# Fetched expert rows of 88 tokens in three sets of 64, 16 and 8: all dots first, then all sums, paced by the product

## The chip, the cores and the metric

The kernel runs on one core of a Trainium2 chip, in one launch. The metric is the device time of that core in microseconds (us), the median of several runs. PE is the matrix engine (TensorE), DVE the vector engine, ACT the scalar engine, POOL the GpSimd engine, which here issues the fetches by index, and SP the engine that issues the large loads. A weight load on PE is listed apart as PEld.

## The reference, cut to what matters

One decoder layer for 256 tokens of width 1024, all in float32: a mixer (attention heads beside recurrent heads), then PEER, then a last norm. The change touches PEER alone. Each token has 8 heads, and each head picks 16 of 16384 experts; an expert is one row of `peer_u` and one of `peer_v`, 4 KB each.

```python
def one(xb):
    qp = (xb @ wq).reshape(PEER_TOKEN_BLOCK, PEER_HEADS, 2, PEER_DKEY // 2)
    s = jnp.einsum('thcd,hcnd->thcn', ...)
    ...
    eidx = jnp.take_along_axis(cidx, p, axis=-1)          # 8 x 16 = 128 rows of each token
    gates = jax.nn.softmax(sc, axis=-1)
    ue = u[eidx]
    ve = v[eidx]
    act = jax.nn.gelu(jnp.einsum('td,thkd->thk', xb, ue), approximate=False)
    return jnp.einsum('thk,thkd->td', (gates * act), ve)
```

The layer ends with `h = h + peer(...)` and `out = rmsnorm(h)`.

## The kernel before

**Two ways for PEER.** 168 of the 256 tokens (`NP`) go the dense way: PE multiplies them with every row of `peer_u` and then of `peer_v`, and a matrix with the gates at the chosen experts (built in the tile `bigB`) picks out what counts. The other 88 tokens (`S`, the first 88) go by fetch: for each, the 128 chosen rows are fetched from memory by index. A fetch (`gissue`) brings 128 rows, one for each partition, 512 KB; 88 fetches bring rows of `peer_u` and 88 rows of `peer_v`, 176 in all.

**The dense stream.** It is a loop of 256 units: units 0 to 127 are the U half (`pu`, from S_U on), units 128 to 255 the V half (`py`, from S_V on). A unit takes one tile of 512 KB (`raw`), which SP loads eight units ahead, and does eight float32 matmuls with it. The trace has two records for each of these, so 16 records are one unit. In the U half ACT takes the results out of PSUM for every second unit with a Gelu (line 1149), one of them for two units. Between units 54 and 116 PE also builds the gate matrix (`gmm`, lines 1131 and 1132).

**The fetched tokens.** They stand in sets of 16 tokens, eight partitions to a token (the last has 8 tokens). For a fetch of kind "u" (`gdo`) DVE multiplies the fetched rows with the token rows (`xr`, loaded by `xload` from the copy `x_keep` in device memory, each row spread to its eight partitions) and adds up to one number for each partition; ACT takes the Gelu of a set's numbers; for a fetch of kind "v" DVE adds the weighted rows to `yacc`. When a set is done, two matmuls with a 0/1 matrix (`gsum`, line 1065) add the partitions of each token together on PE. The list `steps` sets the order: u of set 0, u of set 1, v of set 0, u of set 2, v of set 1, and so on, so a set's token rows are loaded when the set before last has its dots done.

**How the fetches are spread.** `gather(rate)` runs once in each unit. It adds the rate (`GU` 0.8 in the U half, `GV` 0.73 in the V half) to a counter; for every whole one, `gdo` is written for one fetch and `gissue` for the fetch seven places on (`LA` 8). Eight tiles hold fetched rows: four of the pool's tag "gt", four of the tag "sl". The first seven fetches are issued in unit 13 at once. In the V half a fetch also waits for the first matmul of the unit that it is written behind (`PS["pace"]`, a wait of POOL on PE); in the U half it waits for its tile and its turn only.

**The end.** `tail()` at the start of the V half issues four loads on POOL's queue: the residual rows of the dense tokens (three pieces of `h_keep`, into `fin`) and the last norm's vector, spread to all partitions. `gfinish` norms and stores the fetched tokens once the last `gsum` is done. After unit 255 the dense results are copied (`zcopy`), transposed (`ztrans`), normed (`finish`) and stored.

Each engine runs its instructions in the order in which this code writes them.

Of the kernel before, what the change touches and what calls it, by code (L numbers as in the profile page):

```python
# [9 lines left out]
F32 = mybir.dt.float32  # L10
# [3 lines left out]
U32 = mybir.dt.uint32  # L14
AF = mybir.ActivationFunctionType
OP = mybir.AluOpType
# [4 lines left out]
D = 1024  # L21
# [3 lines left out]
TAILN = 2  # L25
S = 88
NP = T - S
NSET = (S + 15) // 16
STEPS = [min(16, S - 16 * m) for m in range(NSET)]
TOP = NP // 2  # L30
R0 = TOP - 45

# [2 lines left out]
def block_kernel(ctx: ExitStack, tc: tile.TileContext, xT, x, lbl, recg, g1, g2, g2f, gf, skT,  # L35
                 w_in, w_out, wq, pu, pv, pur, pvr, out, dbg=None, last_step=None):
    nc = tc.nc
# [24 lines left out]
    S_OUT, S_WQ, S_U, S_V = 28, 36, 52, 180  # L62
    NS = 2 * len(units)
# [77 lines left out]
    for dc in range(8):  # L141
        g = g1t[:, dc:dc + 1]
# [108 lines left out]
    PS = {}  # L251
# [31 lines left out]
    acc = pre.tile([128, 2, 4, 32], F32)  # L283
# [427 lines left out]
    x_keep = dram.tile([128, D], F32)  # L711
# [49 lines left out]
    HN = {}  # L761
# [78 lines left out]
    def routing():  # L840
# [48 lines left out]
        ge = [gm[:, 512 * tt:512 * tt + 128].rearrange("p (n k) -> p n k", k=16) for tt in range(2)]  # L889
# [12 lines left out]
            nc.vector.tensor_mul(ge[tt], ge[tt], gs[tt][:, :, None].to_broadcast([128, 8, 16]))  # L902

        def packed():
            pk = GA["pk"]
            i12 = [PS["I12"][:, r, 0:128].rearrange("p (h a k) -> p h a k", h=8, a=2) for r in range(2)]
            nc.vector.scalar_tensor_tensor(pk[:, :, :, 0:8].bitcast(U32), i12[0], 128.0, i12[1], op0=OP.mult, op1=OP.add)
            nc.vector.tensor_copy(pk[:, :, :, 8:16], ge[0].rearrange("p h (a k) -> p h a k", a=2))
            for m in range(NSET):
                nc.gpsimd.dma_start(GA["pg", m], pk[16 * m:16 * m + STEPS[m]])  # L910
            GA["ready"] = True

        def slots():
# [47 lines left out]
    GA = {}  # L961

    def gather_open():
        gp = PS["gp"]
        GA["pk"] = gp.tile([128, 8, 2, 16], F32, name="pk")
        for m in range(NSET):
            GA["pg", m] = gp.tile([128, 2 * STEPS[m]], F32, name=f"pg{m}")
        GA["dot"] = gp.tile([128, NSET, 16], F32, name="dot")
        GA["w"] = gp.tile([128, NSET, 16], F32, name="gw")
# [4 lines left out]
        nc.vector.tensor_single_scalar(ri, ri, 3, op=OP.logical_shift_right)  # L974
        for n in (16, 8):
            GA["sel", n] = gp.tile([128, 2 * S], F32, name=f"sel{n}")
            nc.vector.tensor_tensor(GA["sel", n], ri, ci, op=OP.is_equal)
            if n == 16:
                nc.vector.tensor_single_scalar(ri, ri, 1, op=OP.logical_shift_right)
        xload(0)  # L980
        xload(1)

    def xload(m):
        if m >= NSET:
            return
        x_ = PS["gp"].tile([128, D], F32, name="xr", bufs=2)
        n = STEPS[m]
        hk = x_keep[16 * m:16 * m + n]
        nc.gpsimd.dma_start(x_, hk[:, None, :].to_broadcast([n, 128 // n, D]))
        GA["x", m] = x_  # L990

    steps = []
    for m in range(NSET):
# [9 lines left out]
    def gissue(j):  # L1003
        if j >= len(steps):
            return
        kind, m, k = steps[j]
        if j % 2:
            g = splp.tile([128, D], F32, name="gt", tag="sl")
        else:
            g = PS["gp"].tile([128, D], F32, name="gt", bufs=4)  # L1010
        i = nc.gpsimd.indirect_dma_start(g, None, pur if kind == "u" else pvr,  # L1011
                                         bass.IndirectOffsetOnAxis(GA["pg", m][:, k // 8 * 16 + k % 8:k // 8 * 16 + k % 8 + 1].bitcast(U32), 0))
        if "pace" in PS:
            tc.add_manual_dep(i.ins, PS["pace"].ins.name, PACE, reason="rows are fetched at the pace of the product")
        GA["g", j] = g

    def gdo(j):
        kind, m, k = steps[j]
        g = GA.pop(("g", j))
        if kind == "u":  # L1020
            x_ = GA["x", m]
            nc.vector.scalar_tensor_tensor(g, g, 1.0, x_, op0=OP.mult, op1=OP.mult,  # L1022
                                           accum_out=GA["dot"][:, m, k:k + 1])
            if k == STEPS[m] - 1:
                GA["gelu"] = [GLAG, m]
                xload(m + 2)
        else:
            w = GA["w"][:, m, k:k + 1]
            if k == 0:
                n = STEPS[m]  # L1030
                nc.vector.tensor_mul(GA["w"][:, m, 0:n].rearrange("p (a k) -> p a k", k=8),
                                     GA["dot"][:, m, 0:n].rearrange("p (a k) -> p a k", k=8),
                                     GA["pg", m].rearrange("p (a f) -> p a f", f=16)[:, :, 8:16])
# [4 lines left out]
            if k == STEPS[m] - 1:  # L1038
                GA["sum"] = [GLAG, m]

    GLAG = 5
# [8 lines left out]
    def gdot():  # L1050
        m = due("gelu")
        if m is not None:
            d = GA["dot"][:, m, 0:STEPS[m]]
            nc.scalar.activation(d, d, AF.Gelu)  # L1054

    def gsum():

        m = due("sum")
        if m is None:
            return  # L1060
        if m == 0:
            GA["p"] = [bank(psG, "pyg") for _ in range(2)]
        y = GA.pop(("y", m))
        for dh in range(2):
            nc.tensor.matmul(GA["p"][dh][0:S], GA["sel", STEPS[m]][:, S - 16 * m:2 * S - 16 * m],  # L1065
                             y[:, dh * 512:dh * 512 + 512], start=m == 0, stop=m == NSET - 1)
        if m == NSET - 1:
            GA["end"] = True

    def gfinish():  # L1070
        f = PS["gp"].tile([128, D], F32, name="fing", tag="xr", bufs=2)
        r = PS["gp"].tile([128, 8], F32, name="rg")
        nc.gpsimd.dma_start(f[0:S], h_keep[0:S, 0])
        jk = PS["gp"].tile([128, D], F32, name="jkg", tag="xr", bufs=2)
        for dh in range(2):
            c = slice(dh * 512, dh * 512 + 512)
            nc.vector.scalar_tensor_tensor(f[0:S, c], GA["p"][dh][0:S], 1.0 / GS, f[0:S, c], op0=OP.mult, op1=OP.add)  # L1077
        nc.scalar.activation(jk[0:S], f[0:S], AF.Square, accum_out=r[0:S, 0:1])  # L1078
        nc.scalar.activation(r[0:S, 1:2], r[0:S, 0:1], AF.Sqrt, bias=epst[0:S], scale=1.0 / D)
        nc.vector.reciprocal(r[0:S, 2:3], r[0:S, 1:2])  # L1080
        nc.vector.scalar_tensor_tensor(f[0:S], f[0:S], r[0:S, 2:3], HN["fin"][0:S, 2], op0=OP.mult, op1=OP.mult)
        nc.gpsimd.dma_start(out[0:S, 0], f[0:S])

    def gather(rate):
        if "ready" not in GA or gpos["do"] >= len(steps):
            return 0.0
# [150 lines left out]
    def pe(s):  # L1237
        if s < S_OUT:
            g, j = divmod(s, 4)
            n = ORD[g]  # L1240
            if n in ("f", "q", "qa", "ka"):
                p = bank(psA if n == "f" else psH, "pp")
# [22 lines left out]
        elif s < S_U:  # L1265
            j = s - S_WQ
            p = bank(psA, "pq")
            mm_col(s, p[:, 0:T], PS["hgH"], PS["hgL"], norm2_mid if j == 0 else None)
            ev(s + 1, ev_qp, j, p)
        elif s < S_V:  # L1270
# [131 lines left out]
```

## Time and profile before

| | |
|---|---|
| median of 3 runs | 841.32 us (840.7 to 842.4) |
| the profiled execution's own time | 845.24 us |
| its span, first to last instruction | 843.5 us |
| PE busy | 817.6 us (97% of the span) |
| DVE, ACT, POOL busy | 507.0, 248.2, 287.2 us |
| moved by DMA | 266.15 MB, 316 GB/s over the span |
| U half, V half on PE | from 197.9 us, from 524.4 us |

Busy time of PE is no measure by itself here, since a matmul that is stretched by a late weight load still counts as busy; the length of a unit tells whether PE is held up. The share of 16 DMA engines and the GB/s are in the same view as the busy times, by stretch.

### The profile page before, as it was taken

Reading aid. Unit: us, or ns where it says so; the run is one execution under the profiler, and the core shown is the slowest. Engines: PE = TensorE matmul, PEld = TensorE weight load, DVE = VectorE, ACT = ScalarE, POOL = GpSimd, SP = SyncE. Lnnn points to the kernel's source line nnn. Section 1 sums busy time; section 2 is a strip of 40 time slices with the busy share of each in tenths; the row PEclk is TensorE's granted clock in tenths of the full one; section 3 lists DMA queues with packets and bytes.
Section 4 is the critical chain, followed back from the end, with each engine's and each line's share of the span. In section 5 each row is a group of like instructions: output and inputs, shape, how many; then the busy total and the mean of one; then the engine's idle time right before and its main releaser. Section 6 shows DMA issues by size and latency. Waiting matters only on the chain.

```text
span 843.5 us, 15460 instructions
## 1 busy us (share of the span) xinstructions
PE 817.6 (97%) x6154; PEld 784.8 (93%) x6154; DVE 507.0 (60%) x1097; ACT 248.2 (29%) x565; POOL 287.2 (34%) x259
## 2 busy tenths in 40 slices
PE   6999999999999999999999999999999999999994
PEld 6987887999989899999999999998999999999994
DVE  6998576499998744777677765434433434334203
ACT  6853854742100214566455521000000000000003
POOL 3053001891284421433324234434533333233001
PEclk9999999999999999999999999999999999999998
DMA  8733335759699999999999999999999999999941
GB/s 312 241 110 102 125 112 191 232 190 325 206 379 409 371 408 408 370 402 370 336 362 338 401 357 382 342 338 409 409 403 407 408 400 401 363 405 402 320 125 50
DMA packets 73655, 266.15 MB, mean 316 GB/s; under 512 B 8751, under 2 KB 8839, under 8 KB 73199
## 3 DMA queue, kind: packets, MB, share of 16 engines
q1 hardware_dynamic: 45470, 164.29, 52.9%
q0 software_dynamic: 27824, 100.87, 31.9%
q8 instruction: 48, 0.79, 0.4%
q14 instruction: 25, 0.20, 0.1%
q10 hardware_dynamic: 288, 0.01, 0.0%
HBM read 262.42 MB, written 2.62 MB: 314 GB/s over the span
## 4 chain that ended last, share of the span: by engine, by line
PE 86%; DMA 7%; DVE 3%; issue 2%; ACT 1%; SPq 0%; ACTq 0%; DVEq 0%
PE pu L1277 33%; PE py L1288 33%; PE pa L214 4%; DMA raw<-in_pv 2%; DMA raw<-in_pu 2%; PE pw L226 2%; PE pq L200 2%; PE pq L201 2%; PE pq L203 2%; DVE sl L80 1%; DMA hT<-in_x 1%; PE pg L1132 1%; PE pyg L1065 1%; PE pg L1131 1%; PE psc L811 1%
## 5 line engine op out<-in xcount | busy, mean ns | idle before, releaser
L1277 PE MATMUL pu<-hn,raw 128*128 128x168 f32 x2048 | 301.5, 307 | 3.6 <-issue 1.6
L1288 PEld LDWEIGHTS py<-bigB,raw 128*128 128x128 f32 x2048 | 292.6, 190 | 9.7 <-DMA raw<-in_pv 6.0
L1288 PE MATMUL py<-bigB,raw 128*128 128x168 f32 x2048 | 298.9, 307 | 2.3 <-DMA raw<-in_pv 1.3
L1277 PEld LDWEIGHTS pu<-hn,raw 128*128 128x128 f32 x2048 | 292.9, 190 | 8.5 <-issue 6.9
L1037 DVE SCALAR_TENSOR_TENSOR yacc<-gt,gw,yacc 128x1024 f32<-128x1024 f32 x82 | 105.2, 1282 | 102.2 <-DMA gt<-in_pvr,pg 102.1
L1011 POOL DMA_INDIRECT gt<-in_pvr,pg x88 | 98.5, 1120 | 180.3 <-PE py L1288 104.5
L1011 POOL DMA_INDIRECT gt<-in_pur,pg x88 | 106.9, 1215 | 143.5 <-DVE gt L1022 48.4
L1022 DVE SCALAR_TENSOR_TENSOR gt<-gt,xr 128x1024 f32<-128x1024 f32 x88 | 106.5, 1222 | 57.0 <-DMA gt<-in_pur,pg 55.2
L1149 ACT ACTIVATE bigB<-pu 128x336 f32<-128x336 f32 (+22 forms) x57 | 21.7, 381 | 161.3 <-PE pu L1277 128.6
L80 DVE TENSOR_TENSOR sl<-raw,sh 128x1024 fp32r<-128x1024 f32 x37 | 52.6, 1427 | 16.9 <-ACT sh L79 16.3
L79 ACT CAST sh<-raw 128x1024 fp32r<-128x1024 f32 x51 | 53.1, 1052 | 14.5 <-PE pw L226 6.0
L1054 ACT ACTIVATE dot<-dot 128x16 f32<-128x16 f32 (+1 forms) x6 | 1.2, 208 | 187.7 <-DVE gt L1022 113.1
L1153 DVE TENSOR_TENSOR bigB<-tmp,bigB 128x336 f32<-128x336 f32 (+22 forms) x37 | 13.2, 357 | 54.0 <-ACT tmp L1152 47.8
L200 PE MATMUL pp<-XH,sh 128*128 128x256 f32 x128 | 32.4, 293 | 6.9 <-ACT sh L150 6.6
L80 POOL TENSOR_TENSOR sl<-raw,sh 128x1024 fp32r<-128x1024 f32 x14 | 33.2, 2388 | 2.2 <-ACT sh L79 2.1
L200 PEld LDWEIGHTS pp<-XH,sh 128*128 128x128 f32 x128 | 25.0, 196 | 7.5 <-ACT sh L150 6.6
L1078 ACT ACTIVATE jkg<-fing 88x1024 f32<-88x1024 f32 x1 | 1.1, 1057 | 104.9 <-DVE fing L1077 104.9
L201 PE MATMUL pp<-XL,sh 128*128 128x256 f32 x128 | 31.7, 288 | 0.0
L200 PE MATMUL pq<-hgH,sh 128*128 128x256 f32 x120 | 29.5, 286 | 0.0
L201 PE MATMUL pq<-hgL,sh 128*128 128x256 f32 x120 | 29.0, 281 | 0.0
L1115 ACT ACTIVATE rt<-iotaC,ni 128x128 f16<-128x128 f16 x88 | 27.6, 400 | 0.0
L201 PEld LDWEIGHTS pp<-XL,sh 128*128 128x128 f32 x128 | 25.1, 196 | 0.5 <-DVE XL L147 0.5
(300 smaller groups left out, 927.2 us busy)
## 6 DMA issues: line engine op xcount, KB each, us to landing
raw<-in_pu SPq DMA_DIRECT2D x128, 512.0 KB
raw<-in_pv SPq DMA_DIRECT2D x128, 512.0 KB
raw<-in_w_in SPq DMA_DIRECT2D x27, 512.0 KB
raw<-in_wq SPq DMA_DIRECT2D x16, 512.0 KB
raw<-in_w_out SPq DMA_DIRECT2D x8, 512.0 KB
xr<-x_keep POOLq DMA_DIRECT2D x6, 512.0 KB
gt<-in_pur,pg POOLq DMA_INDIRECT x88
gt<-in_pvr,pg POOLq DMA_INDIRECT x88
```

The lines of the kernel that those rows point to most:

```text
L79: nc.scalar.copy(h, r)
L80: (nc.gpsimd if s >= S_WQ + 2 else nc.vector).tensor_sub(lo, r, h.bitcast(F32))
L200: nc.tensor.matmul(p, hv[:, dc], xh[:, dc], start=(dc == 0), stop=False)
L201: nc.tensor.matmul(p, hv[:, dc], xl[:, dc], start=False, stop=False)
L214: nc.tensor.matmul(acc[tt], xx[:, dc, tt * 128:(tt + 1) * 128], w[:, c], start=(dc == 0 and w is hv and xx is xh), stop=(dc == 7 and w is lv))
L1011: i = nc.gpsimd.indirect_dma_start(g, None, pur if kind == "u" else pvr, bass.IndirectOffsetOnAxis(GA["pg", m][:, k // 8 * 16 + k % 8:k // ...
L1022: nc.vector.scalar_tensor_tensor(g, g, 1.0, x_, op0=OP.mult, op1=OP.mult, accum_out=GA["dot"][:, m, k:k + 1])
L1037: nc.vector.scalar_tensor_tensor(GA["y", m], g, w, GA["y", m], op0=OP.mult, op1=OP.add)
L1115: nc.scalar.activation(o2[:, k], iotaC, AF.Square, bias=RT["ni"][:, t0 + k:t0 + k + 1])
L1149: nc.scalar.activation(big[:, :, t:NP], p[:, :, t:NP], AF.Gelu)
L1277: nc.tensor.matmul(p, w[:, dc], HN["x"][:, dc], start=dc == 0, stop=dc == 7)
L1288: mm = nc.tensor.matmul(yacc(j), w[:, j * 128:j * 128 + 128], chunk(x), start=x == 0 and j % 2 == 0, stop=x == 127, skip_group_check=True)
```

## The change

There are three sets, of 64, 16 and 8 tokens: a token of the first has two partitions, one of the second eight, one of the third sixteen. The indices and the gates are no longer packed into one tile but sent as two (`pi`, `pg`), three small copies each. `steps` has all 88 dots first (u of sets 0, 1, 2), then all 88 sums (v of sets 0, 1, 2). The token rows of all three sets are loaded when the fetches' tiles are opened, at the start of the U half. Fetches of the U half also wait for the first matmul of their unit. The first seven fetches are issued two in a unit, in units 13 to 16. The rate of the V half is 0.77. `tail()` stands 16 units before the end of the stream.

```diff
-NSET = (S + 15) // 16
-STEPS = [min(16, S - 16 * m) for m in range(NSET)]
+SETS = [64, 16, 8]
+OFFS = [0, 64, 80]
+NSET = len(SETS)
...
             for m in range(NSET):
-                nc.gpsimd.dma_start(GA["pg", m], pk[16 * m:16 * m + STEPS[m]])
+                nc.gpsimd.dma_start(GA["pi", m], ki[OFFS[m]:OFFS[m] + SETS[m]])
+            for m in range(NSET):
+                nc.gpsimd.dma_start(GA["pg", m], kg[OFFS[m]:OFFS[m] + SETS[m]])
             GA["ready"] = True
...
-        xload(0)
-        xload(1)
+        for m in range(NSET):
+            xload(m)

     def xload(m):
-        if m >= NSET:
-            return
-        x_ = PS["gp"].tile([128, D], F32, name="xr", bufs=2)
-        n = STEPS[m]
-        hk = x_keep[16 * m:16 * m + n]
+        x_ = PS["gp"].tile([128, D], F32, name="xr", bufs=3)
+        n = SETS[m]
+        hk = x_keep[OFFS[m]:OFFS[m] + n]
         nc.gpsimd.dma_start(x_, hk[:, None, :].to_broadcast([n, 128 // n, D]))
         GA["x", m] = x_

-    steps = []
-    for m in range(NSET):
-        steps += [("u", m, k) for k in range(STEPS[m])]
-        if m:
-            steps += [("v", m - 1, k) for k in range(STEPS[m - 1])]
-    steps += [("v", NSET - 1, k) for k in range(STEPS[-1])]
+    steps = [(kind, m, k) for kind in "uv" for m in range(NSET) for k in range(SETS[m])]
...
-            if k == STEPS[m] - 1:
+            if k == SETS[m] - 1:
                 GA["gelu"] = [GLAG, m]
-                xload(m + 2)
...
-                GA["y", m] = PS["gp"].tile([128, D], F32, name="yacc", bufs=2)
+                GA["y", m] = PS["gp"].tile([128, D], F32, name="yacc", tag="xr", bufs=3)
...
-            nc.tensor.matmul(GA["p"][dh][0:S], GA["sel", STEPS[m]][:, S - 16 * m:2 * S - 16 * m],
+            nc.tensor.matmul(GA["p"][dh][0:S], GA["sel", m][:, S - OFFS[m]:2 * S - OFFS[m]],
                              y[:, dh * 512:dh * 512 + 512], start=m == 0, stop=m == NSET - 1)
...
     def gather(rate):
         if "ready" not in GA or gpos["do"] >= len(steps):
             return 0.0
-        while gpos["issue"] < min(gpos["do"] + LA - 1, len(steps)):
-            gissue(gpos["issue"])
-            gpos["issue"] += 1
-            if gpos["issue"] == LA - 1:
-                gpos["acc"] = -2.0
+        if gpos["issue"] < LA - 1:
+            for _ in range(2 if gpos["issue"] < LA - 2 else 1):
+                gissue(gpos["issue"])
+                gpos["issue"] += 1
+            if gpos["issue"] < LA - 3:
                 return 0.0
         gpos["acc"] += rate
...
             for dc in range(8):
-                nc.tensor.matmul(p, w[:, dc], HN["x"][:, dc], start=dc == 0, stop=dc == 7)
+                mm = nc.tensor.matmul(p, w[:, dc], HN["x"][:, dc], start=dc == 0, stop=dc == 7)
+                if dc == 0:
+                    PS["pace"] = mm
...
-    GU, GV = 0.8, 0.73
+    GU, GV = 0.8, 0.77
...
-        if s == S_V:
+        if s == NS - 16:
             tail()
```

On POOL, from the opening of the fetches' tiles on, the program before reads so (`xr` are the token rows, `pg` indices and gates, `gt` fetched rows, `fin` what the end needs; "x16" counts equal rows in a run):

```order
L989 DMA xr<-x_keep 128x1x1024 x2
...
L1011 DMA gt<-in_pur,pg_2418 128x1024 x16
L1011 DMA gt<-in_pur,pg_2419 128x1024 x6
L989 DMA xr<-x_keep 128x1x1024
L1011 DMA gt<-in_pur,pg_2419 128x1024 x10
...
L1011 DMA gt<-in_pur,pg_2421 128x1024 x16
L1164 DMA fin<-h_keep 40x1024
L1165 DMA fin<-h_keep 88x1024
L1166 DMA fin<-h_keep 40x1024
L1167 DMA fin<-in_gf 128x1024
L1011 DMA gt<-in_pvr,pg_2420 128x1024 x6
L989 DMA xr<-x_keep 128x1x1024
```

And the same queue in the changed program (its line 992 is `xload`, 1009 `gissue`, 1156 to 1159 `tail`):

```order
L992 DMA xr<-x_keep 128x1x1024 x3
L911 DMA pi_2419<-ki 128x1x64
...
L1009 DMA gt<-in_pur,pi_2419 128x1024 x64
L1009 DMA gt<-in_pur,pi_2423 128x1024 x16
L1009 DMA gt<-in_pur,pi_2427 128x1024 x8
L1009 DMA gt<-in_pvr,pi_2419 128x1024 x64
L1009 DMA gt<-in_pvr,pi_2423 128x1024 x16
L1009 DMA gt<-in_pvr,pi_2427 128x1024 x8
L1156 DMA fin<-h_keep 40x1024
L1157 DMA fin<-h_keep 88x1024
L1158 DMA fin<-h_keep 40x1024
L1159 DMA fin<-in_gf 128x1024
```

Four loads of token rows out of six stood between fetches, and now all three stand ahead of the first; the four loads for the end stood in the middle of the fetches and now stand behind the last.

On PE, from the last part of the U half to the last units, the program before (`pyg` is what `gsum` writes; eight instructions of `pu` or `py` are a unit):

```order
L1277 MATMUL pu<-hn,raw 128x168 x56
L1065 MATMUL pyg<-yacc,sel_2431 88x512 x2
L1277 MATMUL pu<-hn,raw 128x168 x48
L1288 MATMUL py<-bigB,raw 128x168 x296
L1065 MATMUL pyg<-yacc,sel_2431 88x512 x2
L1288 MATMUL py<-bigB,raw 128x168 x352
L1065 MATMUL pyg<-yacc,sel_2431 88x512 x2
L1288 MATMUL py<-bigB,raw 128x168 x256
L1065 MATMUL pyg<-yacc,sel_2431 88x512 x2
L1288 MATMUL py<-bigB,raw 128x168 x88
L1065 MATMUL pyg<-yacc,sel_2434 88x512 x2
L1288 MATMUL py<-bigB,raw 128x168 x20
```

And the changed program:

```order
L1269 MATMUL pu<-hn,raw 128x168 x88
L1282 MATMUL py<-bigB,raw 128x168 x680
L1057 MATMUL pyg<-yacc,sel_2436 88x512 x2
L1282 MATMUL py<-bigB,raw 128x168 x168
L1057 MATMUL pyg<-yacc,sel_2439 88x512 x2
L1282 MATMUL py<-bigB,raw 128x168 x88
L1057 MATMUL pyg<-yacc,sel_2442 88x512 x2
L1282 MATMUL py<-bigB,raw 128x168 x76
```

Six pairs of `pyg` (one more stands earlier in the U half of the program before) are now three, the first of them 85 units into the V half.

## Rows read from the trace of the kernel before

**Rows 1.** The page: busy time, share of the span and instructions of each engine.

```profile
PE 817.6 (97%) x6154; PEld 784.8 (93%) x6154; DVE 507.0 (60%) x1097; ACT 248.2 (29%) x565; POOL 287.2 (34%) x259
```

**Rows 2.** Chain that ended last: start us, us, engine and line, records.

```profile
403.77 1.72 PE pyg L1065 x4
...
616.91 100.32 PE py L1288 x704
...
818.71 1.72 PE pyg L1065 x4
```

**Rows 3.** Instructions of line 1065: durations in ns, first and last start.

```profile
L1065 PE MATMUL pyg<-yacc,sel x24: 592/592/592, 403.6 to 819.8; 128*88 128x512 f32 x24
```

**Rows 4.** Timeline of PE from the start of the V half: start us, us.

```profile
524.44 39.23 PE L1288 MATMUL py<-bigB,raw 128*128 128x168 f32 x272
564.69 2.55 PE L1288 MATMUL py<-bigB,raw 128*128 128x168 f32 x16 [1.02 <-DMA raw<-in_pv]
567.50 47.70 PE L1288 MATMUL py<-bigB,raw 128*128 128x168 f32 x304 [0.26 <-DMA raw<-in_pv]
615.03 1.88 PE L1065 MATMUL pyg<-yacc,sel 128*88 128x512 f32 x4
```

**Rows 5.** Timeline of ACT: the Gelu of every second unit of the U half.

```profile
230.90 0.45 ACT L1149 ACTIVATE bigB<-pu 128x336 f32<-128x336 f32 x1 [4.11 <-PE pu L1277]
...
256.40 0.45 ACT L1149 ACTIVATE bigB<-pu 128x336 f32<-128x336 f32 x1 [3.36 <-issue]
...
283.82 0.45 ACT L1149 ACTIVATE bigB<-pu 128x336 f32<-128x336 f32 x1 [4.11 <-PE pu L1277]
...
320.51 0.45 ACT L1149 ACTIVATE bigB<-pu 128x336 f32<-128x336 f32 x1 [4.68 <-PE pu L1277]
```

**Rows 6.** Stretches: busy us (records) of PE, PEld, DVE, ACT, POOL; clock; DMA share; GB/s.

```profile
198.00:230.00 32.00, 32.00 (x229) 32.00 (x228) 30.94 (x152) 7.91 (x12) 4.48 (x10) 1.00 0.78 250
250.00:280.00 30.00, 30.00 (x213) 30.00 (x212) 25.26 (x94) 3.15 (x7) 14.68 (x15) 1.00 1.03 409
282.00:290.00 8.00, 6.63 (x47) 6.32 (x46) 7.09 (x12) 3.67 (x5) 3.92 (x3) 1.00 1.03 316
530.00:538.00 8.00, 8.00 (x59) 8.00 (x58) 3.82 (x9) 0.22 (x1) 3.28 (x3) 1.00 1.03 265
552.00:564.00 12.00, 11.63 (x80) 11.12 (x78) 3.72 (x3) 0.00 (x0) 5.29 (x4) 1.00 1.04 290
...
524.00:543.00 19.00, 19.00 (x136) 19.00 (x135) 8.70 (x16) 3.44 (x5) 10.57 (x12) 1.00 0.99 322
543.00:616.00 73.00, 71.56 (x466) 66.46 (x466) 29.89 (x32) 0.00 (x0) 30.59 (x21) 1.00 1.03 388
616.00:790.00 174.00, 174.00 (x1211) 172.43 (x1210) 68.57 (x74) 0.42 (x2) 58.56 (x54) 1.00 1.02 397
790.00:825.00 35.00, 35.00 (x232) 32.89 (x231) 3.65 (x5) 2.73 (x4) 0.00 (x0) 1.00 0.52 164
```

**Rows 7.** DMA queues from 250 to 280 us: q1 SP's, q0 POOL's; packets, MB.

```profile
q1 hardware_dynamic: 1678, 6.13, 51.3%
q0 software_dynamic: 1680, 6.11, 51.1%
```

**Rows 8.** Timeline of POOL: issues of loads and fetches.

```profile
272.90 0.57 POOL L989 DMA_DIRECT2D xr<-x_keep  x1 [5.18 <-DVE bigB L860]
...
307.13 0.94 POOL L1011 DMA_INDIRECT gt<-in_pvr,pg  x1 [2.89 <-DVE gt L1022]
326.46 1.15 POOL L1011 DMA_INDIRECT gt<-in_pvr,pg  x1 [18.39 <-DVE gt L1022]
...
526.52 0.60 POOL L1167 DMA_DIRECT2D fin<-in_gf  x1
...
542.06 0.68 POOL L989 DMA_DIRECT2D xr<-x_keep  x1
```

**Rows 9.** Who waited for whom: us in total, times, longest.

```profile
DVE rt L931 <- ACT rt L930: 17.8, 1, 17.8
```

More of the change, by code (lines that the diff above doesn't have):

```diff
@@ L904, in packed @@
         def packed():
[L905 to L908, printed above, removed]
+            ki, kg = GA["ki"], GA["kg"]
+            nc.vector.scalar_tensor_tensor(ki, PS["I12"][:, 0, 0:128], 128.0, PS["I12"][:, 1, 0:128],
+                                           op0=OP.mult, op1=OP.add)
+            nc.vector.tensor_copy(kg, ge[0].rearrange("p h k -> p (h k)"))
             for m in range(NSET):
-                nc.gpsimd.dma_start(GA["pg", m], pk[16 * m:16 * m + STEPS[m]])
+                nc.gpsimd.dma_start(GA["pi", m], ki[OFFS[m]:OFFS[m] + SETS[m]])
+            for m in range(NSET):
+                nc.gpsimd.dma_start(GA["pg", m], kg[OFFS[m]:OFFS[m] + SETS[m]])
             GA["ready"] = True
@@ L964, in gather_open @@
         gp = PS["gp"]
-        GA["pk"] = gp.tile([128, 8, 2, 16], F32, name="pk")
-        for m in range(NSET):
-            GA["pg", m] = gp.tile([128, 2 * STEPS[m]], F32, name=f"pg{m}")
-        GA["dot"] = gp.tile([128, NSET, 16], F32, name="dot")
-        GA["w"] = gp.tile([128, NSET, 16], F32, name="gw")
+        GA["ki"] = gp.tile([128, 128], U32, name="ki")
+        GA["kg"] = gp.tile([128, 128], F32, name="kg")
+        for m, n in enumerate(SETS):
+            GA["pi", m] = gp.tile([128, n], U32, name=f"pi{m}")
+            for k in ("pg", "dot", "w"):
+                GA[k, m] = gp.tile([128, n], F32, name=f"{k}{m}")
         ri = gp.tile([128, 2 * S], I32, name="ri")
@@ L973, in gather_open @@
         nc.gpsimd.iota(ci, pattern=[[1, 2 * S]], base=-S, channel_multiplier=0)
[L974 to L979, printed above, removed]
-        xload(0)
-        xload(1)
-    def xload(m):
-        if m >= NSET:
-            return
-        x_ = PS["gp"].tile([128, D], F32, name="xr", bufs=2)
-        n = STEPS[m]
-        hk = x_keep[16 * m:16 * m + n]
+        at_ = 0
+        for m, n in enumerate(SETS):
+            sh = (128 // n).bit_length() - 1
+            nc.vector.tensor_single_scalar(ri, ri, sh - at_, op=OP.logical_shift_right)
+            at_ = sh
+            GA["sel", m] = gp.tile([128, 2 * S], F32, name=f"sel{m}")
+            nc.vector.tensor_tensor(GA["sel", m], ri, ci, op=OP.is_equal)
+        for m in range(NSET):
+            xload(m)
+    def xload(m):
+        x_ = PS["gp"].tile([128, D], F32, name="xr", bufs=3)
+        n = SETS[m]
+        hk = x_keep[OFFS[m]:OFFS[m] + n]
         nc.gpsimd.dma_start(x_, hk[:, None, :].to_broadcast([n, 128 // n, D]))
         GA["x", m] = x_
-    steps = []
-    for m in range(NSET):
-        steps += [("u", m, k) for k in range(STEPS[m])]
-        if m:
-            steps += [("v", m - 1, k) for k in range(STEPS[m - 1])]
-    steps += [("v", NSET - 1, k) for k in range(STEPS[-1])]
+    steps = [(kind, m, k) for kind in "uv" for m in range(NSET) for k in range(SETS[m])]
     gpos = {"issue": 0, "do": 0, "acc": 0.0}
@@ L1011, in gissue @@
         i = nc.gpsimd.indirect_dma_start(g, None, pur if kind == "u" else pvr,
-                                         bass.IndirectOffsetOnAxis(GA["pg", m][:, k // 8 * 16 + k % 8:k // 8 * 16 + k % 8 + 1].bitcast(U32), 0))
+                                         bass.IndirectOffsetOnAxis(GA["pi", m][:, k:k + 1], 0))
         if "pace" in PS:
@@ L1020, in gdo @@
         if kind == "u":
-            x_ = GA["x", m]
-            nc.vector.scalar_tensor_tensor(g, g, 1.0, x_, op0=OP.mult, op1=OP.mult,
-                                           accum_out=GA["dot"][:, m, k:k + 1])
-            if k == STEPS[m] - 1:
+            nc.vector.scalar_tensor_tensor(g, g, 1.0, GA["x", m], op0=OP.mult, op1=OP.mult,
+                                           accum_out=GA["dot", m][:, k:k + 1])
+            if k == SETS[m] - 1:
                 GA["gelu"] = [GLAG, m]
-                xload(m + 2)
         else:
-            w = GA["w"][:, m, k:k + 1]
+            w = GA["w", m][:, k:k + 1]
             if k == 0:
[L1030 to L1033, printed above, removed]
-                GA["y", m] = PS["gp"].tile([128, D], F32, name="yacc", bufs=2)
+                nc.vector.tensor_mul(GA["w", m], GA["dot", m], GA["pg", m])
+                GA["y", m] = PS["gp"].tile([128, D], F32, name="yacc", tag="xr", bufs=3)
                 nc.vector.tensor_scalar(GA["y", m], g, w, None, op0=OP.mult)
@@ L1037, in gdo @@
                 nc.vector.scalar_tensor_tensor(GA["y", m], g, w, GA["y", m], op0=OP.mult, op1=OP.add)
-            if k == STEPS[m] - 1:
+            if k == SETS[m] - 1:
                 GA["sum"] = [GLAG, m]
@@ L1052, in gdot @@
         if m is not None:
-            d = GA["dot"][:, m, 0:STEPS[m]]
-            nc.scalar.activation(d, d, AF.Gelu)
+            nc.scalar.activation(GA["dot", m], GA["dot", m], AF.Gelu)
     def gsum():
@@ L1070, in gfinish @@
     def gfinish():
-        f = PS["gp"].tile([128, D], F32, name="fing", tag="xr", bufs=2)
+        f = PS["gp"].tile([128, D], F32, name="fing", tag="xr", bufs=3)
         r = PS["gp"].tile([128, 8], F32, name="rg")
         nc.gpsimd.dma_start(f[0:S], h_keep[0:S, 0])
-        jk = PS["gp"].tile([128, D], F32, name="jkg", tag="xr", bufs=2)
+        jk = PS["gp"].tile([128, D], F32, name="jkg", tag="xr", bufs=3)
         for dh in range(2):
```

## The prediction

> **What bounds the kernel now.** I read the page first: PE is busy for 97% of the span and no other engine for more than 60% [rows 1]. So time can only come from three places: work taken off PE, units that last longer than PE needs for them, and what follows the last unit. The granted clock is 1.00 in every stretch of the stream [rows 6], so all matmuls run at the upper of the two levels and the clock plays no part.
>
> Then the chain of waits gives the length of an undisturbed unit: 704 records, 44 units, in 100.32 us, which is 2.28 us each [rows 2]. Against that I held the stretches. In the V half, from 524.44 to the matmuls of the sum at 615.03, PE has 272 + 16 + 304 = 592 records, 37 units [rows 4]. They should last 84.4 us and last 90.6, so 6.2 us are lost, at waits for `raw`. After that the half runs at 2.28. In the U half the Gelu of every second unit should come every 4.56 us. From 283.82 to 320.51 seven intervals last 36.7 us in place of 31.9, a loss of 4.8; from 230.90 to 256.40 five last 25.5 in place of 22.8, a loss of 2.7 [rows 5]. All else in the stream is PE at its pace.
>
> Why `raw` is late shows in the DMA rows. From 250 to 280 us the 16 DMA engines are full (share 1.03) and move 409 GB/s [rows 6]. In that stretch SP's queue and POOL's queue move 6.13 and 6.11 MB [rows 7]: with work waiting in both, each gets half, 204 GB/s. A unit's 0.524 MB in 2.28 us is 230 GB/s. So PE eats its stock of loaded tiles as long as fetches are waiting, and once it is gone a unit lasts 0.524 MB / 204 GB/s = 2.56 us; the row of 16 records at 564.69 has 2.55 [rows 4].
>
> Some stretches don't even reach 409. From 282 to 290 it is 316, from 530 to 538 it is 265, from 552 to 564 it is 290, with the DMA engines as full [rows 6]. Each of them comes some microseconds after POOL has issued a load of token rows (272.90 and 542.06) or of the end's vectors (526.52) [rows 8]. These are the loads from the copies `x_keep` and `h_keep`, or of the same 4 KB for many partitions. I take them as the cause; the rows show only the coincidence, three times out of three.
>
> **The change part by part.**
>
> Sums on PE: a pair of matmuls per set takes 1.72 us on the chain [rows 2], and 24 records, four to a pair, make six pairs [rows 3]. Three remain. The engine that sets the end does 3 x 1.72 = 5.2 us less.
>
> The V half: the four loads of the end and the token rows of the sixth set leave it. They were 1.21 MB (296 rows of 4 KB) and 0.52 MB in POOL's queue, and besides they took the two slow stretches with them: (409 - 265) GB/s x 8 us + (409 - 290) x 12 = 2.6 MB not moved. Without these 4.3 MB nothing is left that pushed the half into its stall, if the new rate leaves room: a unit now asks for (1 + 0.77) x 0.524 MB = 0.928 MB in 2.28 us, 407 GB/s, against 409 measured [rows 6]. At 0.73 it was 398. It fits, narrowly, so I count the whole 6.2 us. The lower bound is nothing (rival B).
>
> The U half: the third load of token rows (272.90) goes from between the fetches to ahead of them. That takes 0.52 MB and the slow stretch of 282 to 290, (409 - 316) x 8 us = 0.74 MB, out of the time in which the two queues share. Half of 1.27 MB is SP's: 0.63 MB, 1.2 tiles, 1.2 x 2.28 = 2.8 us of stall. The number of fetches does not fall: by unit 52 the loop has issued 7 + 0.8 x 36, about 36, as before, so the queues still share for most of that stretch. The pace on PE holds POOL back only where it ran ahead. Bounds: nothing, and the whole 4.8 + 2.7 = 7.5 us. I take 2.8, since it is the part that has rows, and 2.7 of the 7.5 stand where no wait is shown.
>
> At no cost I count: the third load of token rows at the start of the U half, because from 198 to 230 us PE is busy throughout and the DMA engines move only 250 GB/s [rows 6]; were that cover gone, one 0.52 MB load is a unit, 2.3 us. The loads of the end, which now come 16 units before the stream's end, when the fetches are over: from 790 to 825 the DMA engines are half idle (0.52) [rows 6], and 1.21 MB at the 164 GB/s that they move there take 7 us of 36; late, they would hold up the last norms one for one. Dots and sums on DVE, of which there are as many as before on an engine at 60% [rows 1]. The added wait on PE in the U half: behind a waiting fetch on POOL stand only further fetches, and the one who waits for them is DVE, at the dot seven fetches on, 7 / 0.8 = 8.75 units or 20 us later. A fetch in a shared queue takes 2.56 us of it, and after the opening burst five or six are waiting, about 14 us. That is under 20 (rival D).
>
> The sum: 845.2 (the profiled execution's own time) - 5.2 - 6.2 - 2.8 = 831.0 us. The median of the runs lies 3.9 us under the profiled one, 841.3 to 845.2, and I carry that over: **827 us**, 1.7% less.
>
> **The rivals.**
>
> A, the sum above: the sums' 5.2 us and the V stall go, part of the U stall. 824 to 831 us.
>
> A+, the U half loses all its stalls, because DMA work is spread by the pace: 7.5 in place of 2.8. 822 us. For it speaks that a hole follows POOL's run ahead (a fetch at 307.13, the next at 326.46 [rows 8]), which the pace fills; against it, that the same fetches must pass before unit 52.
>
> B, the higher rate takes back what the loads gave: 2 GB/s of room in place of 11. From 616 to 790 us the mean was 397 [rows 6], though at a demand of 398. If 397 is all that can be had, a unit of the V half lasts 0.928 / 397 = 2.34 us; 176 fetches less the 97 issued by its start (7 + 0.8 x 112) leave 79, at 0.77 these are 103 units, and 103 x 0.06 = 6 us, the whole of that gain. 841.3 - 5.2 - (0 to 2.8) = 833 to 836 us.
>
> C, slower: the V half becomes DMA-bound outright, at unit 128 and for those 103 units. From 524 to 616 us the rows give (322 x 19 + 388 x 73) / 92 = 374 GB/s [rows 6]. At that a unit lasts 2.48 us and 103 of them 20.6 us more: 841.3 - 14.2 + 20.6 = 848 us. It decides from 384 GB/s down, where 103 x 0.138 eats the 14.2. Against it: those 92 us hold the two slow stretches that go away, and 409 stood for 30 us. The Trainium skill speaks for it: its page "DMA: Bandwidth & Descriptors", section "Bandwidth", says that for transfers from device memory into the core's memory a limit of some 358 GB/s per core binds, under the fabric's 435. By that rule a unit would last 2.59 us and the estimate would be 859 us. The trace disagrees with it: it moves 409 GB/s for 30 us, and I go by the trace.
>
> D, the routing on DVE comes late. Before, DVE ran ahead: before unit 52 it stood waiting for 17.8 us for PE's transposes to pass [rows 9]. Now a dot can't be done before its paced fetch lands, and the routing behind it on DVE's queue waits too. If fetches take 25 us in place of 14, PE waits some 5 us at the transposes, and once more after a further slow spell: 832 to 840 us. It would be slower than before only from 34 us on.
>
> **How the numbers follow.** A 0.60, A+ 0.10, B 0.16, C 0.07, D 0.07. The prediction is A's 827 us. The range of 822 to 836 takes in A, A+, B and the better half of D, and leaves C and the rest out, less than 2 in 10. Runs of this kernel differ by 0.2% (840.7 to 842.4), which is 1.7 us: A, A+, B and most of D are faster by more, C is slower; what remains is spread between. Faster 0.90, same 0.03, slower 0.07.
>
> **What would show it.** In the changed kernel's profile: 12 records of the sum's matmuls in place of 24; units of 2.28 us from 128 on, with no wait for `raw` near unit 144; no stretch under 350 GB/s in the V half while fetches run; the slow stretch of the token rows between 200 and 215 us with PE busy through it; the Gelus of the U half still over 4.56 us apart somewhere between units 30 and 52, but fewer of them; POOL's waits for PE in the U half too, and no long hole; the V half's fetches over by unit 231. I am wrong if V units are above 2.28 us under a full DMA (B, C), if PE waits for DVE near unit 52 (D), or if the slow stretches appear again without those loads.

## The result and the profile after

The changed kernel takes 828.04 us (median of 4 runs, 826.98 to 829.41) where the kernel before took 841.22 beside it (840.7 to 842.4): ratio 0.9842, 95% interval 0.9825 to 0.986. Its profiled execution took 828.13 us, almost its median, with a span of 826.3 us. The profiled execution of before lay 3.9 us over its median, so the two traces differ by 17.2 us of span where the medians differ by 13.2.

The page's busy times, against [rows 1]:

```profile
PE 805.7 (98%) x6142; PEld 782.8 (95%) x6142; DVE 509.6 (62%) x1095; ACT 244.2 (30%) x560; POOL 282.0 (34%) x256
```

The chain that ended last, from the end of the U half on (start us, us, engine and line, records), answers to [rows 2, 4]. The V half has no piece in it but PE:

```profile
515.41 193.80 PE py L1282 x1360
709.21 1.72 PE pyg L1057 x4
710.92 47.88 PE py L1282 x336
758.80 1.72 PE pyg L1057 x4
760.52 25.08 PE py L1282 x176
785.60 1.72 PE pyg L1057 x4
```

1360 records are 85 units, and 193.80 us are 2.28 us each. The three pairs of the sum, 1.72 us each, are all that remains of six.

The stretches of the changed kernel (busy us and records of PE, PEld, DVE, ACT, POOL; clock; DMA share; GB/s), against [rows 6]:

```profile
204.00:218.00 14.00, 14.00 (x100) 14.00 (x100) 13.31 (x70) 4.62 (x7) 0.00 (x0) 1.00 1.03 280
250.00:280.00 30.00, 30.00 (x213) 30.00 (x212) 24.04 (x102) 2.78 (x7) 13.15 (x11) 1.00 1.03 409
282.00:290.00 8.00, 8.00 (x58) 8.00 (x57) 6.82 (x20) 3.48 (x5) 3.99 (x4) 1.00 1.03 410
552.00:616.00 64.00, 64.00 (x452) 64.00 (x451) 28.31 (x22) 0.00 (x0) 26.19 (x23) 1.00 1.03 409
616.00:750.00 134.00, 134.00 (x935) 132.94 (x934) 56.90 (x47) 0.00 (x0) 49.48 (x44) 1.00 1.02 405
754.00:768.00 14.00, 14.00 (x92) 12.94 (x91) 2.23 (x2) 0.00 (x0) 0.00 (x0) 1.00 1.04 303
```

From 282 to 290 us the DMA engines now move 410 GB/s in place of 316, and the V half, from 552 us on, runs at 405 to 409 in place of 388 and 397. The slow stretches have not vanished but moved: 280 GB/s at 204 to 218 us, after the three loads of token rows, and 303 at 754 to 768, after the end's loads. PE is busy through both.

The Gelus of the U half on ACT, against [rows 5]:

```profile
231.39 0.45 ACT L1141 ACTIVATE bigB<-pu 128x336 f32<-128x336 f32 x1 [4.11 <-PE pu L1269]
...
254.19 0.45 ACT L1141 ACTIVATE bigB<-pu 128x336 f32<-128x336 f32 x1 [4.11 <-PE pu L1269]
...
281.61 0.45 ACT L1141 ACTIVATE bigB<-pu 128x336 f32<-128x336 f32 x1 [4.11 <-PE pu L1269]
...
314.05 0.45 ACT L1141 ACTIVATE bigB<-pu 128x336 f32<-128x336 f32 x1 [4.67 <-PE pu L1269]
319.17 0.45 ACT L1141 ACTIVATE bigB<-pu 128x336 f32<-128x336 f32 x1 [4.67 <-PE pu L1269]
```

Five intervals last 22.80 us, exactly 4.56 each (25.5 before). Seven, from 281.61 to 314.05, last 32.44, and the eighth 5.12: a loss of 0.5 + 0.6 us where 4.8 were lost before. The wait list has POOL held by PE in the U half, and a shorter wait of the routing, against [rows 9]:

```profile
POOL gt L1009 <- PE pu L1269: 133.3, 66, 4.7
...
DVE rt L934 <- ACT rt L933: 9.1, 1, 9.1
```

For sums over a half I take the first record of each unit (16 records). From unit 1 to unit 128 the trace of before has 323.4 us and that of after 313.7; from 128 to 254 it is 300.4 and 292.4. Less the pairs of the sum that went (two in the U half, one in V), the U half gave 6.2 us and the V half 6.2. With 5.2 for the three pairs that is 17.6; 0.5 was lost ahead of unit 1.

### The profile page after: what moved, and what is told of

It is laid out like the page before. It is cut to its first block, busy times and chain, and to the rows that moved or that the text cites. A ratio compares the mean times of both kernels' runs of the same rounds, so it can differ in the third digit from the quotient of the medians.

```text
span 826.3 us, 15423 instructions
## 1 busy us (share of the span) xinstructions
PE 805.7 (98%) x6142; PEld 782.8 (95%) x6142; DVE 509.6 (62%) x1095; ACT 244.2 (30%) x560; POOL 282.0 (34%) x256
## 4 chain that ended last, share of the span: by engine, by line
PE 90%; DVE 4%; DMA 2%; issue 2%; ACT 1%; SPq 0%; ACTq 0%; DVEq 0%
PE pu L1269 36%; PE py L1282 35%; PE pa L215 4%; PE pw L227 2%; PE pq L201 2%; PE pq L202 2%; PE pq L204 2%; DVE sl L81 2%; DMA hT<-in_x 1%; PE pg L1124 1%; PE pg L1123 1%; PE psc L812 1%; DMA raw<-in_w_in 1%; PE pw L240 1%; PE pyg L1057 1%
## 5 line engine op out<-in xcount | busy, mean ns | idle before, releaser
L1269 PE MATMUL pu<-hn,raw 128*128 128x168 f32 x2048 | 298.2, 307 | 0.3
L1282 PE MATMUL py<-bigB,raw 128*128 128x168 f32 x2048 | 294.0, 306 | 0.8 <-DVE zt L1166 0.8
L1030 DVE SCALAR_TENSOR_TENSOR yacc<-gt,w,yacc 128x1024 f32<-128x1024 f32 x85 | 109.2, 1285 | 130.7 <-DMA gt<-in_pvr,pi 130.4
L1009 POOL DMA_INDIRECT gt<-in_pvr,pi x88 | 101.2, 1150 | 161.5 <-PE py L1282 121.1
L1009 POOL DMA_INDIRECT gt<-in_pur,pi x88 | 100.6, 1144 | 156.2 <-PE pu L1269 117.5
L1141 ACT ACTIVATE bigB<-pu 128x336 f32<-128x336 f32 (+24 forms) x58 | 22.2, 382 | 159.8 <-PE pu L1269 159.8
L1145 DVE TENSOR_TENSOR bigB<-tmp,bigB 128x336 f32<-128x336 f32 (+24 forms) x36 | 13.2, 367 | 50.6 <-ACT tmp L1144 50.5
L335 POOL TENSOR_TENSOR dd<-cum 128x1024 f32<-128x1024 f32 x5 | 11.1, 2229 | 41.5 <-DVE cum L315 36.3
```

The source lines that it names most:

```text
L1141: nc.scalar.activation(big[:, :, t:NP], p[:, :, t:NP], AF.Gelu)
L1269: mm = nc.tensor.matmul(p, w[:, dc], HN["x"][:, dc], start=dc == 0, stop=dc == 7)
L1282: mm = nc.tensor.matmul(yacc(j), w[:, j * 128:j * 128 + 128], chunk(x), start=x == 0 and j % 2 == 0, stop=x == 127, skip_group_check=True)
```

## The experiments

The experiments ran in three groups, each on one chip. First group, where the kernel before took 840.75 us: the changed kernel without the pace, with the end's loads early in two forms, and with the pairs twice. Second group, 846.58 us: before with the pace, with distinct rows and with the end's loads late, and the changed kernel at a rate of 0.90. Third group, 845.61 us: the changed kernel at 0.73, with the old opening and with a stepped rate, and before with the new opening. So ratios to before are given, and times are compared within a group. Stalls are what units last over 2.28 us, added up over units 14 to 24, over 30 to 51, and over the V half; what PE spends in them on other matmuls (the sums, the gate matrix and 0.7 us for `psl`, the routing's transposes, which fall in one of the units 49 to 52) is taken off. A stall is read from one profiled execution, a time from 4 to 25 runs.

**The pace left out of the U half.**

```diff
-                mm = nc.tensor.matmul(p, w[:, dc], HN["x"][:, dc], start=dc == 0, stop=dc == 7)
-                if dc == 0:
-                    PS["pace"] = mm
+                nc.tensor.matmul(p, w[:, dc], HN["x"][:, dc], start=dc == 0, stop=dc == 7)
```

> The changed kernel without the wait for PE in the U half; nothing else differs. In the profile the U half of the changed kernel loses 1.5 us to units over 2.28 us, where that of before lost 7.5. My theory gives the gain to the token rows that left the stretch: then 828 us as with the pace, within 1 us, and U stalls of 1 to 3 us in the profile. Rival: the pace gives it, because without it POOL issues fetches up to eight units ahead and SP's queue has to share: then POOL shows a hole again near unit 52, the units lengthen well before unit 40, and the time is 831 to 834 us.

827.39 us (826.22 to 829.07), ratio 0.9835 (0.9815 to 0.9856). The U half lasts 313.9 us against 313.7, with the same stalls in units 47 to 51. The pace is not what freed the U half: the reason given for rival A+ falls.

**The pace put into the U half of the kernel before** (the same three lines added there).

> The program before with one part of the change: fetches of the U half wait for the first matmul of their unit, too. My theory: the third load of token rows and its slow stretch stay, so most of the U stalls stay, 839 to 841 us. Rival, that the pace gives the U half's gain: U stalls under 2 us and 836 to 838 us.

843.26 us, ratio 0.9949 (0.9929 to 0.9969). The profiled execution (845.37, the longest of its 12) has 4.9 us of stall in units 30 to 51, much as before (5.2), and a V stall of 6.6. So the rival's sign, U stalls under 2 us, is not there, but a gain of 0.3 to 0.7% is measured, which is as much as the rival's time. Its place is not in the one trace; it stays open.

**The end's loads back at the start of the V half, in the changed kernel.**

```diff
-        if s == NS - 16:
+        if s == S_V:
             tail()
```

> The changed kernel with the four loads of the end back at the start of the V half. They are 1.21 MB in POOL's queue and bring a slow stretch. If they alone made the V stall of 6.2 us, the time is 834 us. My estimate is less: POOL's queue is behind by 1.21 MB and half of what a slow stretch fails to move, SP's queue has to share until that is made up, and the stock of some four loaded tiles takes most of it: units over 2.28 us for 0 to 2 us, 828 to 830 us. A slow stretch at 265 to 300 GB/s should show just after the loads. Rival: the stall came from the token rows' load alone: no slow stretch, 828 us.

830.79 us (829.41 to 831.62), ratio 0.9873 (0.9853 to 0.9892), 3.4 us over the kernel without the pace in the same group. The V half stalls again, 1.7 us in units 156 to 162, and the U half lasts 0.5 us longer. In the chain, 464 records are 29 units of 2.28 us, and then units last 2.55:

```profile
516.39 66.17 PE py L1282 x464
...
582.57 5.09 PE py L1282 x32
...
587.67 2.55 PE py L1282 x16
```

**The same, with the four loads reading distinct rows of `peer_u`** (for three loads from `h_keep` and one row spread to all partitions).

```diff
-nc.gpsimd.dma_start(f[0:128 - S, 0], h_keep[S:128, 0])
+nc.gpsimd.dma_start(f[0:128 - S, 0], pur[S:128])
 ...
-nc.gpsimd.dma_start(f[:, 2], bass.AP(tensor=gf.tensor, offset=gf.offset, ap=[[0, 128], [1, D]]))
+nc.gpsimd.dma_start(f[:, 2], pur[256:384])
```

> As the run with the loads of the end at the start of the V half, but these four read as many different rows of the expert table, not the copy of the residual and not one row for 128 partitions. The last norm's inputs are left out by that, so the output is not the reference's. My theory, that those sources make the slow stretch: the stretch after the loads stays above 390 GB/s, no V unit over 2.28 us, 828 us. Rival, that any additional load makes it slow: the stretch and the time as with the real sources.

831.04 us, ratio 0.9876 (0.9856 to 0.9897): no gain, and its trace has 3.2 us of V stall. The stretch behind these loads is still slow, with the DMA engines full:

```profile
516.00:520.00 4.00, 4.00 (x31) 4.00 (x30) 3.89 (x4) 2.08 (x4) 3.69 (x6) 1.00 1.03 396
520.00:526.00 6.00, 6.00 (x45) 6.00 (x44) 4.41 (x4) 0.00 (x0) 2.98 (x4) 1.00 1.03 255
526.00:540.00 14.00, 14.00 (x101) 14.00 (x100) 3.11 (x4) 0.00 (x0) 4.87 (x5) 1.00 1.03 399
```

For the end's loads the source was the wrong suspect.

**The kernel before with all loads of token rows and of the end reading distinct rows of `peer_u`** (the four loads of the end are changed as in the run above).

```diff
-        nc.gpsimd.dma_start(x_, hk[:, None, :].to_broadcast([n, 128 // n, D]))
+        nc.gpsimd.dma_start(x_, pur[512 + 128 * m:640 + 128 * m])
```

> The program before, its bytes and places unchanged, but the loads of token rows and of the end read as many different rows of the expert table; the dots and the last norm then have wrong inputs and the output is not the reference's. If the slow stretches come from the sources, there is none in this profile, and what is left of the V stall is the bytes' part: an estimate of 0 to 2 us, 834 to 837 us. If the bytes make the stall, 841 us with the same units near 144. Rival for the cause of the slow stretches: they stay where they were.

839.96 us, ratio 0.9931 (0.9908 to 0.9955). Its stretches:

```profile
282.00:290.00 8.00, 8.00 (x56) 7.72 (x56) 7.90 (x14) 3.87 (x5) 4.75 (x4) 1.00 1.03 408
...
527.00:534.00 7.00, 7.00 (x51) 7.00 (x51) 4.23 (x9) 0.22 (x1) 2.68 (x3) 1.00 1.03 267
...
552.00:564.00 12.00, 12.00 (x86) 12.00 (x85) 4.58 (x4) 0.00 (x0) 4.55 (x5) 1.00 1.03 409
```

With the same bytes, the two slow stretches behind token rows are gone (408 and 409 GB/s, for 316 and 290 in [rows 6]), and the one behind the end's loads stays at 267. So 4 KB rows read by several partitions each, from the copy, are what made the first two slow; the two properties were changed together. The stalls of units 30 to 51 fall to 3.4 us, and the V half lasts 296.5 us, 3.9 less, with 2.4 us of stall left.

**The end's loads late, in the kernel before, nothing else.**

```diff
-        if s == S_V:
+        if s == NS - 16:
             tail()
```

> The program before with one part of the change: the four loads of the end stand 16 units before the end of the stream. The token rows still come between fetches. If the V stall of 6.2 us needs both loads, because the stock of loaded tiles takes up one of them, the stall goes and the time is 835 us. If each load costs its share, half goes and it is 838 us. Rival: those loads had no part, 841 us.

842.04 us, ratio 0.9955 (0.993 to 0.998). In the chain the stall of [rows 4] is gone, though the token rows and their slow stretch are still there (342 GB/s from 543 to 552 us, 358 from 552 to 564):

```profile
524.61 84.36 PE py L1288 x592
608.97 1.72 PE pyg L1065 x4
```

37 units in 84.36 us are 2.28 each: in this trace one of the two reliefs was enough for the whole 6.2 us. It is the fastest of 12 executions (839.01 to 847.85), and the medians of its chip differ by 4.5 us (846.58 and 842.04), so that other executions may well keep part of the stall.

**Each pair of the sum done twice, in the changed kernel.**

```diff
-        for dh in range(2):
-            nc.tensor.matmul(GA["p"][dh][0:S], ..., start=m == 0, stop=m == NSET - 1)
+        for rep in range(2):
+            for dh in range(2):
+                nc.tensor.matmul(GA["p"][dh][0:S], ..., start=m == 0 and rep == 0,
+                                 stop=m == NSET - 1 and rep == 1)
```

> The changed kernel with each set's pair of sum matmuls run twice, three more pairs as in the program before; each sum counts twice in the output, which is not the reference's. If the pairs count one for one on the engine that sets the end, 3 x 1.72 us more: 833.2 us, with units otherwise the same. Rival: a waiting DMA hides them (the stock of tiles fills while PE sums), 828 to 830 us.

832.76 us, ratio 0.9899 (0.988 to 0.9918), 5.4 us over the kernel without the pace in the same group. In the chain a set now takes 3.43 us:

```profile
708.43 3.43 PE pyg L1058 x8
711.87 47.88 PE py L1284 x336
```

The V half is 5.15 us longer, three pairs of 1.72: they count one for one.

**A rate of 0.90 in the V half of the changed kernel**, with the end's loads 24 units earlier (behind the fetches again).

```diff
-    GU, GV = 0.8, 0.77
+    GU, GV = 0.8, 0.90
 ...
-        if s == NS - 16:
+        if s == NS - 40:
             tail()
```

> The changed kernel with a rate of 0.90 in the V half, which asks for 1.9 x 0.524 MB in a unit, 437 GB/s at 2.28 us; the loads of the end stand 40 units before the stream's end, as the fetches are over earlier. By 409 GB/s a unit then lasts 2.44 us once the stock is used up; 79 / 0.9 = 88 units, 14 us, less some 5 us of stock: 836 to 838 us. By the page DMA: Bandwidth & Descriptors of the Trainium skill (section Bandwidth), a limit of some 358 GB/s per core, a unit would last 2.78 us, by which the estimate is over 860 us; no other number here hangs on that. Rival: the fetches just fall behind and PE keeps 2.28 us, 828 us.

842.6 us, ratio 0.9954 (0.9934 to 0.9973), which is 0.0112, or 9.4 us, above the changed kernel's ratio; beside the 841.22 us of before this ratio is 837.4 us, within the 836 to 838 expected. Its V half:

```profile
530.00:600.00 70.00, 70.00 (x491) 69.64 (x490) 35.15 (x28) 0.00 (x0) 34.19 (x28) 1.00 1.03 409
600.00:700.00 100.00, 99.63 (x643) 91.73 (x642) 47.01 (x39) 0.00 (x0) 47.37 (x37) 1.00 1.03 409
```

Here DMA is the bound: units 163 to 200 last 2.49 us on average, and the rate is 409 GB/s for 170 us. The trace has 11.5 us of V stall, 2.0 of them in units 218 to 222, behind the end's loads. That settles rival C: 409 is what these transfers get for as long as they ask for it. The limit of some 358 GB/s per core that the Trainium skill gives (page "DMA: Bandwidth & Descriptors", section "Bandwidth") is not what holds here. The same section of the Trainium skill calls some 358 GB/s the share of each core when both cores of a memory domain stream. This kernel runs on one core; the prediction and the expectation of this run took the limit without that condition.

**The rate of 0.73 in the changed kernel.**

```diff
-    GU, GV = 0.8, 0.77
+    GU, GV = 0.8, 0.73
```

> The changed kernel with the rate of the V half put back from 0.77 to 0.73 fetches per unit; nothing else. Theory (407 GB/s asked of 409 fits, so that the higher rate neither costs nor gives anything while PE sets the pace): a ratio to the kernel before of 0.984, the same as the changed kernel within 0.002, all units of the V half 2.28 us. Rival 1 (the higher rate already costs in the V half): faster than the changed kernel by over 0.002. Rival 2 (the higher rate gives something, since the fetches are over sooner): slower by over 0.002; at 0.73 the fetches end some 6 units later, by unit 236 or so, and the end's loads at unit 238 then stand right behind them.

830.79 us, ratio 0.9813 (0.9786 to 0.9841). The interval overlaps that of the changed kernel, which did not run on this chip; the times alone can't place it within 0.002. The trace can, for the V half:

```profile
517.60 205.20 PE py L1282 x1440
722.80 1.72 PE pyg L1057 x4
```

90 units of 2.28 us, and 292.4 us for the half, as at 0.77. The rate neither costs nor gives there.

**The old opening in the changed kernel**: seven fetches at once in unit 13, as in the kernel before (the expectation says unit 16, but the first is issued at 232.45 us and unit 16 starts at 234.7).

```diff
-        if gpos["issue"] < LA - 1:
-            for _ in range(2 if gpos["issue"] < LA - 2 else 1):
-                gissue(gpos["issue"])
-                gpos["issue"] += 1
-            if gpos["issue"] < LA - 3:
+        while gpos["issue"] < min(gpos["do"] + LA - 1, len(steps)):
+            gissue(gpos["issue"])
+            gpos["issue"] += 1
+            if gpos["issue"] == LA - 1:
+                gpos["acc"] = -2.0
                 return 0.0
```

> The changed kernel with the opening of the kernel before: seven fetches at once at unit 16, and two units' worth of credit taken off, in place of two fetches per unit. Theory (the 6 us that the U half gave came from the opening: a burst of 3.7 MB in POOL's queue empties the stock of landed weight tiles, and PE stands at unit 17 or 18): the stall at units 17 and 18 is back, 2 to 3 us, and the stalls before unit 52 begin at unit 38 or so in place of 47, 1 to 4 us more; ratio to before 0.988 to 0.990. Rival (the opening doesn't matter; the loads of token rows that left the U half were the cause): no stall at unit 17 or 18, ratio 0.984.

829.21 us (827.44 to 831.2), ratio 0.9796 (0.9769 to 0.9822).

**The new opening in the kernel before** (the same block the other way round).

> The kernel before with the opening of the changed one: two fetches per unit until seven are under way, in place of seven at once. Everything else as before (six sets of 16, third load of token rows between the fetches, loads of the end at the start of the V half, rate 0.73). Theory (the opening is the cause of the U half's 6 us): no stall at units 17 and 18, the stalls before unit 52 begin some 8 units later, the U half shorter by 3 to 6 us; ratio 0.993 to 0.997. Rival (the loads are the cause): the U half's stalls as in the kernel before, ratio 0.998 to 1.002.

845.85 us, ratio 0.9999 (0.9977 to 1.0021). The U half is as before: seven intervals of the Gelu last 37.2 us, 5.3 over 31.9, where [rows 5] lost 4.8:

```profile
282.46 0.45 ACT L1149 ACTIVATE bigB<-pu 128x336 f32<-128x336 f32 x1 [4.11 <-PE pu L1277]
288.30 0.45 ACT L1149 ACTIVATE bigB<-pu 128x336 f32<-128x336 f32 x1
...
319.63 0.45 ACT L1149 ACTIVATE bigB<-pu 128x336 f32<-128x336 f32 x1 [4.67 <-PE pu L1277]
```

These two were to show that the opening freed the U half, a theory formed after the first two groups, in which units 17 and 18 had a gap in the three variants with the burst and in none without. It falls: with the burst the changed kernel keeps its small stalls (1.7 us in units 30 to 51), and without it the kernel before keeps its large ones (6.1). The four runs of the table that carry the third load of token rows between the fetches as it was, and no other, lose 4.9 us or more there:

| stall, us | units 14 to 24 | units 30 to 51 |
|---|---|---|
| before | 2.7 | 5.2 |
| before, end's loads late | 1.5 | 5.3 |
| before, with the pace | 0.8 | 4.9 |
| before, new opening | 1.1 | 6.1 |
| before, distinct rows | 1.8 | 3.4 |
| changed, and seven variants of it | 0 to 1.4 | 1.4 to 2.1 |
| changed, rate 0.90 (same U half as changed) | 0 | 3.5 |

**The changed kernel with the rate in three steps.**

```diff
-        st["acc"] -= gather(GU if s < S_V else GV)
+        st["acc"] -= gather(0.72 if s < S_U + 56 else 0.9 if s < S_U + 118 else GV)
```

> The changed kernel with the rate of fetches in three steps: 0.72 per unit up to unit 56, while weight tiles are prefetched behind a small stock; 0.9 from there to unit 118, where the trace has full units and room; 0.77 after. Theory (the 1.5 us of stalls that the changed kernel still has between units 47 and 55 come from fetches that share the DMA engines while the stock is small; fewer of them there leave none, and the later ones fit): no unit over 2.35 us between 16 and 56, total 1 to 2 us less than the changed kernel, ratio 0.982. Rival (0.9 per unit asks 437 GB/s of 409 and eats the stock, so that units after 80 or those at the start of the V half last longer): ratio 0.985 or more.

828.83 us, ratio 0.9784 (0.9756 to 0.9812). Against the others of its group it is 0.4 us under the one with the burst and 2.0 under the one at 0.73. Its trace does not show the gain that was meant: units 38 to 41 still stall, 1.4 us in all, and unit 18 has a gap of 1.1. The V half did not suffer (292.4 us). That it beats the changed kernel is not shown.

## Why the prediction was right

**The sums** (5.2 us): right in size and place. The chain has three pairs, and doubling them cost 5.15 us.

**The V half** (6.2 us): right in size. Units last 2.28 us at a demand worked out as 407 GB/s, and 405 to 409 were moved. But the terms were counted as if all 4.3 MB had to leave. In the traces, the end's loads alone, moved late, give the whole 6.2 us; with them left in and the rest of the change made, 1.7 come back, so that the rest alone is worth 4.5; with distinct rows in place of the spread ones, 3.9 go. These parts add up to more than 6.2. That fits PE drawing on loaded tiles first, with a stall only when they are gone: before, PE ran 39.23 us into the half without a wait [rows 4].

**The U half** (2.8 us): the term was mis-sized, and its mechanism fits but was not tested by itself. In units 30 to 51 the trace of before loses 5.2 us and that of after 1.4, so 3.8 went, 1.0 more than the sum "Half of 1.27 MB is SP's" gave. For the third load of token rows and its slow stretch speaks that the four traces with that load as it was lose 1.8 to 2.5 us in units 37 to 39, in or right behind the slow stretch, where the one with distinct rows loses 0.6 and the changed kernel and its variants 0 to 0.9. But no run moved this load alone. The opening, tried each way round, is not the cause. The pace gives nothing in the changed kernel, though before it gave 0.5% whose place is not known. How the 3.8 us split between the slow stretch and the load's bytes is open too: distinct rows were traced once (3.4 left), and the changed U half alone loses between 1.4 and 3.5 us from trace to trace.

Most of the rest of the 6.2 us between the two traces is the gap in units 17 and 18, 2.7 us before and none after. The prediction noted that no wait is shown there, and that holds: the timeline of PE before has

```profile
240.02 0.54 PE L1277 MATMUL pu<-hn,raw 128*128 128x168 f32 x2 [0.19 <-issue]
240.76 0.52 PE L1277 MATMUL pu<-hn,raw 128*128 128x168 f32 x2 [0.21 <-issue]
242.20 0.44 PE L1277 MATMUL pu<-hn,raw 128*128 128x168 f32 x2 [0.92 <-issue]
```

gaps between single matmuls of one unit, with nothing that releases them. It is no wait for `raw`, which would stand at a unit's start. A gap there or two units later came in all four variants of the third group, with and without the burst, and in none of the first. What makes it is open.

**The 3.9 us** between the profiled execution and the median: this step failed too. It was carried over as if it would stay, but the changed kernel's profiled execution is its median. The excess may have been stalls which the change removed: both traces together give 6.2 + 6.2 us of stall, 3.4 more than the 9.0 that the sum counted, and the medians 13.2 - 5.2 = 8.0. It may also have been the chip: the profiled execution of before is none of the timed ones (840.7 to 842.4), and its 845.24 us lie by the 846.58 and 845.61 that the same kernel took on two other chips; on which one it ran is not on record. Either way an under-sized U half and a correction too many met at 827, and the agreement within 1 us owes much to luck.

**At no cost**: right. The three loads of token rows at 204 to 218 us and the end's loads at 754 to 768 lie under a busy PE. The last fetch was issued at 750.24 us, in unit 230 (by unit 231 was worked out), and the end's loads stood right behind it.

**The rivals.** B and C need the V half short of DMA: at 0.77 it is not, at 0.90 it is. D needs PE to wait for the routing: the wait of DVE that [rows 9] had at 17.8 us is 9.1, and PE shows no wait for it. A+ named the pace, which gives nothing in the changed kernel (and 0.5% in the one before, where most of the U stalls stay).

## What to carry to other kernels

Where two queues share full DMA engines, add up what each asks for in the time in which PE runs through its stock of loaded tiles; a load that is small against the whole decides there, and costs nothing some tens of microseconds away. Reliefs of one stall don't add: price them one at a time and stop at the stall's size. Where the profiled execution lies outside the timed runs, its distance to the median is no offset that every version keeps: it can be stalls that come and go, or another chip.

## What was not expected

- Loads of token rows that give one 4 KB row to several partitions pull all transfers down, to 290 to 316 GB/s for 8 to 12 us, with the DMA engines as full; as many bytes in distinct rows don't (408 and 409). The end's loads do so with either source (255 to 267 GB/s), for a reason that stays open. SP's own transfers, whose source is the same throughout, slow down with them: one of its packets takes 147 ns on average from 250 to 280 us and 189 from 282 to 290 in the kernel before (51.3% and 50.7% of 16 engines' time, for 1678 and 344 packets).
- 409 GB/s into the core is held for 170 us when asked for.
- The same kernel before took 840.75, 846.58 and 845.61 us on three chips, while the changed kernel's variants at rates of 0.73 and 0.77 lay between 827.4 and 832.8. The change is worth some 13 us on one and 16 on another (829.21 with the burst against 845.61).
